# PSUM banks given back at their last reading, one pool for slabs and temporaries, and activation tables asked for early

## The chip, the cores and the metric

The kernel runs on one core of a Trainium2 chip. The metric is the time of one execution in microseconds of the device; three runs of the kernel before gave 800.99, 803.68 and 805.22, median 803.68 us. The core has TensorE (PE in the profile; PEld is its weight load), VectorE (DVE), ScalarE (ACT), GpSimd (POOL) and SyncE (SP), which issues nearly all transfers here. Products land in PSUM, which has eight banks of 128 x 512 fp32; everything else is held in SBUF.

## The reference

Two layers of a decoder trunk over 256 tokens of width 1024, fp32 in and out:

```
for i in range(2):
    h = rms_norm(x, norm_mix[i])
    x = x + (dsa_moba_mixer(h, ...) if i == 0 else nsa_mixer(h, ...))
    x = x + memory_cross_attention(rms_norm(x, norm_mem[i]), rms_norm(mem, norm_mem_src[i]), ...)
    x = x + swiglu(rms_norm(x, norm_ffn[i]), ffn_w_in[i], ffn_w_out[i])
```

- Mixer of layer 0: one projection of 2472 columns. Half A: an indexer of 8 small ReLU heads scores all causal keys, each query keeps its best 64, and 8 heads attend to those with one shared key and value head. Half B: 8 heads of plain causal attention (with 256 tokens there is one block). Queries and keys are RMS-normed per head and turned by rotary angles in 16 of 64 columns.
- Mixer of layer 1: 16 heads in 4 groups, three branches (15 compressed blocks, selected blocks, a window), each with its own keys and values, mixed by sigmoid gates; then an output projection.
- Memory attention: 4 heads of 128 columns over 256 memory rows. Feed-forward: SiLU(g) * u with 2816 columns.

## The kernel before

Tokens stand in two tiles of 128 (`t` = 0, 1). All large products are done in three passes of fp32r: `mm3` multiplies high by high, high by low and low by high part, so that one fp32 product has three TensorE instructions per 128 rows of the sum. Weights come in blocks of 256 x 512 fp32 (`raw`, three buffers), ScalarE or VectorE rounds them to a high part, and VectorE subtracts it for the low part (`whl`, six buffers).

Nothing is in a fixed order. Every step of the computation is a generator that yields one operation at a time (`Op`) or a condition; `Steps.run` collects the operations that are ready, asks a model of the engines (`Est`) when each could start, and issues the one that could start first, with a small window (`WAIT`) in which rank and age decide. So the instruction order of each engine is the outcome of a planner. What moves an instruction is when its generator is let on (a buffer or a flag) and what the model believes of durations and of the TensorE clock.

Buffers are `Slots`: a tile is taken with `get` (which waits until one is open) and given back by calling the function that came with it. PSUM has four such sets of two banks: `MM` (`mm`, the large products), `SP` (`sp`, scores), `TP` (`tp`, transposes) and `PV` (`po`, values). In SBUF there are 23 slabs (`SL`), and of temporaries four `T2` (`t2`), two `T4`, three `SN` (`sn`, scores), four `PT` (`pt`, transposed scores) and two `GV` (`gv`); `T2` and `T4` both read `t` in the profile. Giving back is the planner's act: on the chip the next writer of a bank waits by semaphore for its last reader, whenever the planner gave it back.

`gemm` takes a bank of `MM`, issues the product and starts an evacuation `ev`. The evacuations of queries and keys (`ev_q`, `ev_k`, `ev_sw`) copy the bank to a temporary and then run `inv_rms`, whose first step squares the bank on ScalarE:

```
yield move(q.rearrange("p h d -> p (h d)"), ps)
yield from inv_rms(ps, 8, HD, (yield from root("mix0", t))[0], 1.0, HD, rq[j, t])
free()
```

`inv_rms` goes on to a sum on VectorE, a scale-and-add on VectorE and a power on GpSimd; the bank is given back after these.

In layer 0 the products come in the order `s` (indexer, shared key and value), `aq`, `bk`, `bq`, `bv`, then `mk` (memory keys) and `out`; in layer 1 `kc`, `ks`, `kw`, `vw`, `q0`, `q1`, then `mk` and `out`. The attention generators run beside them. `tables` computes the rotary sines and cosines (`ang`, `sin`, `cos`) and the norm gains that TensorE spreads over the partitions in one small product. In the profile all instructions of an engine's helper are on line 238, so tiles tell them apart, not lines.

Of the kernel before, what the change touches and what calls it, by code (L numbers as in the profile page):

```python
# [53 lines left out]
NSLAB = 23  # L54
TAPS = 8
PTS = 4


class Op:
# [81 lines left out]
class Est:  # L141


    def __init__(self, nc):
        self.clk = {"PE": 0.0, "V": 0.0, "S": 0.0, "G": 0.0, "D": 0.0, "port": 0.0}
        self.wr, self.rd, self.busy = {}, {}, {}
        self.thin = False
        self.now = 0.0
        self.eng = {n: Est.Engine(self, n, e) for n, e in
                    (("PE", nc.tensor), ("V", nc.vector), ("S", nc.scalar), ("G", nc.gpsimd))}  # L150
# [44 lines left out]

    def issue(self, e, outs, ins, cost):
        lock = self.locks(e, outs, ins)
        t = max(self.clk[e], self.after(e, outs, ins), self.clk["port"] if lock else 0.0)
        if e == "PE":
            w = int(t / 3.413)  # L200
            c = cost * (1 if self.busy.get(w - 1, 0.0) > 1.26 else 2)
            n = 1
            for d in outs[0].shape[1:]:
                n *= d
# [12 lines left out]
        for a in outs:  # L217
            self.note(a, self.wr, t, e)

    class Engine:  # L220
# [3 lines left out]
        def __getattr__(self, name):  # L224
            f = getattr(self.e, name)

            def call(*a, **k):
                aps = [v for v in (*a, *k.values()) if hasattr(v, "tensor")]
                outs, ins = [aps[0]], aps[1:]
                if name == "tensor_tensor_reduce":  # L230
                    outs.append(aps[-1])
                    ins = aps[1:-1]
                elif k.get("accum_out") is not None:
                    outs.append(k["accum_out"])
                    ins = [v for v in ins if v is not k["accum_out"]]

                def do():
                    return f(*a, **{q: v() if q in ("start", "stop") and callable(v) else v for q, v in k.items()})  # L238
                return Op(self.est, [(self.n, outs, ins, self.cost(name, a, k, outs, ins), do)])
            return call  # L240

        def cost(self, name, a, k, outs, ins):
# [56 lines left out]

@with_exitstack  # L300
def trunk(ctx: ExitStack, tc: tile.TileContext, I, out):
# [37 lines left out]
    spawn = ck.spawn  # L339
    MM, SP, TP, PV = Slots(est, pp, "mm", 2), Slots(est, pp, "sp", 2), Slots(est, pp, "tp", 2), Slots(est, pp, "po", 2)  # L340
# [131 lines left out]
    PO.memset(one, 1.0).issue()  # L472
    mhalf = cp.tile([P, 16], F32, name="mhalf")
# [18 lines left out]
    def tables():  # L492
# [20 lines left out]
        yield S.activation(cos, ang, AF.Sin)  # L513
        yield has(("mix0", 0), 2)
# [254 lines left out]
    def mixer0():  # L769
# [119 lines left out]
        def ev_k(ps, free, t):  # L889
# [3 lines left out]
            yield from inv_rms(ps, 8, HD, (yield from root("mix0", t))[0], 1.0 / HD, 1.0, rk)  # L893
            free()
# [98 lines left out]
    def mixer1():  # L993
# [92 lines left out]
        def ev_sw(br):  # L1086
            def ev(ps, free, t):
# [7 lines left out]
                free()  # L1095
# [28 lines left out]
        def ev_q(j):  # L1124
            def ev(ps, free, t):
                q, qf = yield from T2.get([P, 8, HD])
                yield move(q.rearrange("p h d -> p (h d)"), ps)
                yield from inv_rms(ps, 8, HD, (yield from root("mix1", t))[0], 1.0, HD, rq[j, t])
                free()
# [160 lines left out]
    def mem_k(L):  # L1290
# [3 lines left out]
        def ev(ps, free, t):  # L1294
# [3 lines left out]
            yield from inv_rms(ps, MH, MD, mvr[t][0], 1.0 / MD, 1.0, rk)  # L1298
            free()
# [15 lines left out]
    def mem_attn(L):  # L1315
        vm = hp.tile([P, NT, MH, MD], F32, name="mvm")
        qT, rq = {}, [hp.tile([P, MH], F32, name=f"mrq{t}") for t in range(NT)]

        def ev_q(ps, free, t):
            q, qf = yield from T2.get([P, MH, MD])  # L1320
            yield S.activation(q.rearrange("p h d -> p (h d)"), ps, AF.Copy)
            yield from inv_rms(ps, MH, MD, (yield from root(("mem", L), t))[0], 1.0, MD, rq[t])
            free()
# [20 lines left out]
        def mem_pv(t, p, sp, spf, sn, snf):  # L1344
# [20 lines left out]
            for i in range(2):  # L1365
                yield together([T.matmul(po[:, i, :], vm[:, b, h0 + i, :], pt[:, 2 * i + b, :], start=(b == 0), stop=(b == 1))
                                for b in range(2)])
            ptf()
            hl, hf = yield from SL.get([P, 2, 2, P], F32R)
# [4 lines left out]
        def ev_v(p):  # L1374
            def ev(ps, free, t):
                yield move(vm[:, t, 2 * p:2 * p + 2].rearrange("p h d -> p (h d)"), ps, mvr[t][1])
# [183 lines left out]
```

## Time and profile before

| | us |
|---|---|
| median of three runs | 803.68 |
| profiled execution | 802.33 |
| its span on the core | 800.6 |
| TensorE busy | 765.6 (96%) |
| VectorE busy | 533.0 (67%) |
| ScalarE busy | 436.7 (55%) |
| GpSimd busy | 132.8 (17%) |
| SyncE's queue moved | 120.5 MB |

The profile's span leaves out 1.7 us around the program. The page gives for each engine how long it worked; the stretches give the same between two times, with the clock granted to TensorE as a share of full speed; the timeline gives instructions in order, with the idle time ahead of them and what ended it. An engine's idle time matters where it is on the path that sets the end.

### The profile page before, as it was taken

The numbers are of one execution on the slowest core, as the hardware profiler recorded it, in microseconds if no ns is written. First come the engines' busy times: TensorE is split into PE (matmuls) and PEld (weight loads), VectorE is DVE, ScalarE is ACT, GpSimd is POOL, SyncE is SP. The second block draws the span as 40 slices with busy tenths as digits, with TensorE's granted clock in tenths as the row PEclk, the third lists the DMA queues.
The fourth block names the chain that finished last, engine by engine and source line by source line (L and its number), as shares of the span: only waits on it lengthen the run. The fifth ranks groups of instructions, "written<-read, shape, count | busy, mean of one in ns | idle before, by whom it ended". The sixth has DMA issues, their size and how long they took to land.

```text
span 800.6 us, 11834 instructions
## 1 busy us (share of the span) xinstructions
PE 765.6 (96%) x4259; PEld 635.5 (79%) x4259; DVE 533.0 (67%) x1088; ACT 436.7 (55%) x822; POOL 132.8 (17%) x194
## 2 busy tenths in 40 slices
PE   6988999999999999999998988999999999999998
PEld 5766788897888889788877767887897888889886
DVE  6888998868555554554726888886857565546541
ACT  5766985675543443443615677884656344435430
POOL 1665340100000000000016373340200000000000
PEclk9998999999999999999999998999999999999999
DMA  7633643426556645876414623033624665546751
GB/s 221 192 98 92 194 136 100 142 102 193 166 171 206 186 156 157 228 247 186 131 46 123 212 78 106 2 105 108 188 102 132 211 187 183 160 140 212 218 189 52
DMA packets 69482, 121.27 MB, mean 151 GB/s; under 512 B 8420, under 2 KB 15664, under 8 KB 69424
## 3 DMA queue, kind: packets, MB, share of 16 engines
q1 hardware_dynamic: 69392, 120.53, 48.8%
q8 instruction: 33, 0.54, 0.3%
q14 instruction: 25, 0.20, 0.1%
q0 software_dynamic: 32, 0.00, 0.0%
HBM read 119.46 MB, written 1.05 MB: 151 GB/s over the span
## 4 chain that ended last, share of the span: by engine, by line
PE 78%; DVE 8%; ACT 5%; DMA 5%; issue 2%; POOL 1%; SPq 0%; ACTq 0%; DVEq 0%; POOLq 0%
PE mm L238 58%; PE po L238 11%; PE tp L238 7%; PE sp L238 2%; DVE whl L238 2%; DVE slab L238 1%; ACT whl L238 1%; DMA raw<-in_ffn_w_in 1%; DMA raw<-in_ab_w_in 1%; ACT sn L238 1%; DMA raw<-in_nsa_w_in 1%; ACT slab L238 1%; DVE sn L238 1%; DVE kvT L238 1%; DVE hss L238 1%
## 5 line engine op out<-in xcount | busy, mean ns | idle before, releaser
L238 PE MATMUL mm<-whl,h 128*128 128x512 f32 (+3 forms) x1776 | 399.1, 379 | 10.1 <-DVE whl L238 9.1
L238 PEld LDWEIGHTS mm<-whl,h 128*128 128x128 f32 x1776 | 311.8, 189 | 69.9 <-DVE whl L238 10.9
L238 DVE TENSOR_TENSOR whl<-raw,whl 128x1024 fp32r<-128x1024 f32 (+3 forms) x232 | 271.3, 1174 | 143.3 <-ACT whl L238 139.0
L238 ACT ACTIVATE whl<-raw 128x1024 fp32r<-128x1024 f32 (+2 forms) x212 | 214.7, 1016 | 167.4 <-DMA raw<-in_ffn_w_in 42.0
L238 PE MATMUL mm<-whl,slab 128*128 128x512 f32 (+1 forms) x840 | 198.6, 375 | 2.0 <-ACT mvm L238 1.0
L238 PEld LDWEIGHTS mm<-whl,slab 128*128 128x128 f32 x840 | 141.7, 188 | 28.3 <-DVE x L238 1.8
L238 PE MATMUL po<-whl,slab 128*128 128x512 f32 x264 | 68.2, 396 | 0.0
L238 POOL TENSOR_TENSOR rh<-vh,mhalf 128x1 f32<-128x1 f32 x12 | 10.1, 845 | 326.7 <-DVE vh L238 310.5
L238 ACT ACTIVATE slab<-tp 128x256 fp32r<-128x256 f32 (+2 forms) x72 | 31.3, 463 | 50.9 <-PE tp L238 50.8
L238 PEld LDWEIGHTS po<-whl,slab 128*128 128x128 f32 x264 | 49.3, 188 | 11.4
L238 ACT ACTIVATE sn<-sn,mx 128x128 f32<-128x128 f32 (+1 forms) x96 | 42.7, 448 | 6.2 <-DVE mx L238 5.8
L238 POOL TENSOR_TENSOR sn<-sn,rc 128x512 f32<-128x512 f32 (+2 forms) x32 | 32.6, 1022 | 48.9 <-DVE rc L238 30.8
L238 PE MATMUL tp<-ident,t 128*128 128x128 f32 x224 | 35.5, 282 | 4.4 <-DVE slab L238 2.9
L238 PEld LDWEIGHTS tp<-ident,t 128*128 128x128 f32 x224 | 27.3, 143 | 11.8 <-POOL t L238 3.2
L238 DVE CUSTOM_DVE_ANT_0 sn<-sp,cm,rq 128x128 f32<-128x128 f32 (+1 forms) x80 | 30.6, 409 | 7.8 <-PE sp L238 6.6
L238 PE MATMUL tp<-ident,sn 128*128 128x128 f32 (+1 forms) x180 | 31.6, 288 | 2.1 <-POOL sn L238 1.4
L238 ACT ACTIVATE pt<-tp 128x512 f32<-128x512 f32 (+2 forms) x51 | 26.8, 535 | 11.7 <-PE tp L238 11.1
L238 DVE TENSOR_TENSOR x<-mm,x 128x512 f32<-128x512 f32 x36 | 24.5, 686 | 13.0 <-PE mm L238 12.9
L238 ACT ACTIVATE h<-gv 128x512 fp32r<-128x512 f32 x22 | 13.8, 628 | 30.9 <-DVE gv L238 30.9
L238 ACT ACTIVATE t<-mm,rh 128x512 f32<-128x512 f32 (+1 forms) x26 | 17.0, 654 | 24.7 <-PE mm L238 24.7
L238 ACT ACTIVATE t<-mm 128x512 f32<-128x512 f32 (+2 forms) x44 | 23.1, 557 | 9.1 <-PE mm L238 6.9
L238 PEld LDWEIGHTS tp<-ident,sn 128*128 128x128 f32 (+1 forms) x180 | 21.8, 146 | 7.5 <-POOL sn L238 2.3
(198 smaller groups left out, 667.9 us busy)
## 6 DMA issues: line engine op xcount, KB each, us to landing
raw<-in_ffn_w_in SPq DMA_DIRECT2D x80, 512.0 KB, 3.9
raw<-in_ffn_w_out SPq DMA_DIRECT2D x44, 512.0 KB, 4.4
raw<-in_ab_w_in SPq DMA_DIRECT2D x16, 512.0 KB, 3.7
raw<-in_mem_w_kv SPq DMA_DIRECT2D x16, 512.0 KB, 3.8
raw<-in_nsa_w_in SPq DMA_DIRECT2D x16, 512.0 KB, 4.1
raw<-in_ab_w_out SPq DMA_DIRECT2D x8, 512.0 KB, 3.7
raw<-in_mem_w_q SPq DMA_DIRECT2D x8, 512.0 KB, 3.8
raw<-in_mem_w_o SPq DMA_DIRECT2D x8, 512.0 KB, 4.1
```

Of the source, the lines that this page charges most:

```text
L238: return f(*a, **{q: v() if q in ("start", "stop") and callable(v) else v for q, v in k.items()})
```

## The change

1. `inv_rms` gets the bank's `free` and calls it right after the square; in `ev_sw` the copy of the values is put ahead of it.
2. Slabs, `T2`, `SN`, `PT` and `GV` share one pool of 36 places of 2 KB. Each kind has a least number (23, 4, 3, 2, 1) that stays reserved for it; what is over goes to who asks first. The values of the memory attention (`mvm`, 4 KB of their own) now take two places.
3. A one-column activation with Sin is issued in the set-up, and one with Exp right behind the cosine.
4. The planner's model: ScalarE is charged 1.28 us when its table changes, the TensorE clock is believed to follow plain busy time, and an fp32 product of 64 x 64 weights is charged 0.235 us.

```
 class Op: issue
+        if e == "S":
+            self.est.load(getattr(f, "func", None))
         self.est.issue(e, outs, ins, cost)
 class Est
+    def load(self, func):
+        table = {AF.Sin: "sin", AF.Exp: "exp", AF.Silu: "silu"}.get(func)
+        if table not in (None, self.table):
+            self.table = table
+            self.clk["S"] += 1.28
     issue, TensorE
             c = cost * (1 if self.busy.get(w - 1, 0.0) > 1.26 else 2)
-            self.busy[w] = self.busy.get(w, 0.0) + cost * ins[0].shape[0] / P * min(1.0, n / P)
+            self.busy[w] = self.busy.get(w, 0.0) + cost
     cost, TensorE
+                if ins[0].shape[0] == 64 and outs[0].shape[0] == 64:
+                    return 0.235
+class Kind:
+    def ready(self):
+        p = self.p
+        if p.used[self.k] < p.least[self.k]:
+            return True
+        return len(p.slots.open) > sum(max(0, p.least[k] - p.used[k]) for k in p.least)
...
-    SL = Slots(est, hp, "slab", NSLAB)
-    T2, T4, SN, PT = Slots(est, tp, "t2", 4), Slots(est, tp, "t4", 2), Slots(est, tp, "sn", 3), Slots(est, tp, "pt", PTS)
-    GV = Slots(est, tp, "gv", 2)
+    places = Places(est, hp, "place", PLACES, LEAST)
+    SL, T2, SN, PT, GV = (places.kind(k) for k in LEAST)
+    T4 = Slots(est, tp, "t4", 2)
...
+    S.activation(warm, one, AF.Sin).issue()
...
         yield S.activation(cos, ang, AF.Sin)
+        yield from ready(AF.Exp)
...
-    def inv_rms(ps, H, dh, v, mul, add_k, r):
+    def inv_rms(ps, H, dh, v, mul, add_k, r, free):
         sq, f = yield from T2.get([P, H, dh])
         yield S.activation(sq.rearrange("p h d -> p (h d)"), ps, AF.Square)
+        free()
...
     ev_q of layer 0 (ev_k, ev_q of layer 1, mem_k and mem_attn alike)
-                yield from inv_rms(ps, 8, HD, (yield from root("mix0", t))[0], 1.0, HD, rq[j, t])
-                free()
+                yield from inv_rms(ps, 8, HD, (yield from root("mix0", t))[0], 1.0, HD, rq[j, t], free)
     ev_sw
-                yield from inv_rms(ps[:, :256], G, HD, v, 1.0 / HD, 1.0, rk[:, :G])
                 if br == 0:
                     yield S.activation(vv[:, t, :G, :], ps[:, 256:].rearrange("p (h d) -> p h d", h=G), AF.Copy, scale=r)
-                free()
+                yield from inv_rms(ps[:, :256], G, HD, v, 1.0 / HD, 1.0, rk[:, :G], free)
     mem_attn
-        vm = hp.tile([P, NT, MH, MD], F32, name="mvm")
+        vm = {}
...
+                if p == 0:
+                    vm[t] = yield from SL.get([P, MH, MD])
+                yield lambda: t in vm
```

The order moves on all engines in the two mixers; the same instructions stand in the same order in the feed-forward blocks. TensorE in layer 0, from the end of the second `bq` product to the `bv` product, before (`mm_753` and `mm_876` are these two products, `t_798`, `t_859` and `t_821` hold keys and a memory row tile):

```order
L238 MATMUL mm_753<-whl_689,h_113 128x512 x2
L238 MATMUL mm_753<-whl_689,h_114 128x512
L238 MATMUL tp_816<-ident,t_798 128x128 x4
L238 MATMUL tp_849<-ident,t_798 128x128 x4
L238 MATMUL tp_861<-ident,t_859 128x128 x4
L238 MATMUL mm_876<-whl_734,h_111 128x512 x2
```

Now, the same two products are `mm_764` and `mm_832`, the keys `t_804`:

```order
L245 MATMUL mm_764<-whl_696,h_115 128x512 x2
L245 MATMUL tp_812<-ident,t_804 128x128 x4
L245 MATMUL mm_764<-whl_696,h_116 128x512
L245 MATMUL mm_764<-whl_696,h_115 128x512 x2
L245 MATMUL mm_764<-whl_696,h_116 128x512
L245 MATMUL mm_832<-whl_736,h_113 128x512
L245 MATMUL tp_842<-ident,t_804 128x128 x4
```

The transposes that stood between the two products stand inside them.

TensorE in layer 1, where the first memory-key product (`mm_5104`, now `mm_5442`) sets in among the attention (`tp`, `po`, `sp`), before:

```order
L238 MATMUL tp_5063<-ident,sn_4989 128x128
L238 MATMUL po_4757<-pt_5041,vv 64x128 x4
L238 MATMUL po_4757<-pt_4987,vv 64x128 x4
L238 MATMUL tp_5063<-ident,sn_4989 128x128 x3
L238 MATMUL mm_5104<-whl_4462,slab_4969 128x512 x2
```

And now:

```order
L245 MATMUL tp_5382<-ident,place_5290 128x128
L245 MATMUL po_5264<-place_5376,vv 64x128 x4
L245 MATMUL po_5017<-place_5317,vv 64x128 x4
L245 MATMUL mm_5442<-whl_4483,place_5296 128x512
L245 MATMUL sp_5435<-place_4173,place_5187 128x256
```

From the last instruction of the `q1` products to this point 162 instructions stand without a product before, and 234 now; inside the second `q1` product 24 stood before and 81 stand now, so more of the attention is ahead of `mk`.

ScalarE at the sine and the cosine, before:

```order
L238 ACTIVATE whl_273<-raw_223 128x1024
L238 ACT_TABLE_LOAD
L238 ACTIVATE sin<-ang 128x16
L238 ACTIVATE whl_297<-raw_233 128x1024
L238 ACTIVATE t_304<-mm_241 128x424
L238 ACTIVATE sqk,ssk<-mm_241 128x64
L238 ACTIVATE cos<-ang 128x16
L238 ACTIVATE whl_314<-raw_271 128x1024
```

And now:

```order
L245 ACTIVATE sin<-ang 128x16
L245 ACTIVATE whl_299<-raw_235 128x1024
L245 ACTIVATE place_306<-mm_243 128x424
L245 ACTIVATE sqk,ssk<-mm_243 128x64
L245 ACTIVATE cos<-ang 128x16
L245 ACT_TABLE_LOAD
L245 ACTIVATE warm<-one 128x1
L245 ACTIVATE whl_354<-raw_297 128x1024
```

The load moves from ahead of the sine to behind the cosine; one conversion (`whl_314`) has gone to VectorE. Before, another load stands ahead of the first Exp of the attention; now none does. ScalarE has five loads in all for six.

## Rows read from the trace of the kernel before

**Rows 1.** The page: busy us (share) xinstructions of each engine; chain that ended last.

```profile
PE 765.6 (96%) x4259; PEld 635.5 (79%) x4259; DVE 533.0 (67%) x1088; ACT 436.7 (55%) x822; POOL 132.8 (17%) x194
...
PE 78%; DVE 8%; ACT 5%; DMA 5%; issue 2%; POOL 1%; SPq 0%; ACTq 0%; DVEq 0%; POOLq 0%
```

**Rows 2.** Stretches: length; TensorE, loads, VectorE, ScalarE, GpSimd busy (x); clock; DMA share, GB/s.

```profile
0.00:28.00 28.00, 19.07 (x84) 15.89 (x85) 18.98 (x59) 15.31 (x28) 5.53 (x14) 1.00 0.72 219
28.00:84.00 56.00, 48.69 (x240) 38.02 (x238) 48.34 (x135) 38.56 (x69) 33.63 (x60) 0.94 0.41 120
84.00:100.00 16.00, 15.91 (x94) 13.21 (x94) 15.71 (x52) 15.01 (x36) 5.97 (x6) 1.00 0.61 192
100.00:420.00 320.00, 318.24 (x1749) 263.43 (x1749) 200.63 (x332) 162.68 (x278) 22.39 (x32) 1.00 0.53 160
420.00:458.18 38.18, 33.07 (x195) 28.50 (x193) 28.95 (x60) 21.90 (x42) 17.82 (x29) 1.00 0.54 164
458.18:466.91 8.73, 8.73 (x53) 7.23 (x51) 7.18 (x27) 6.69 (x23) 8.65 (x11) 1.00 0.56 183
466.91:498.55 31.64, 25.07 (x213) 21.52 (x213) 25.93 (x96) 24.19 (x73) 14.16 (x19) 0.84 0.25 84
498.55:546.40 47.85, 47.79 (x394) 40.24 (x394) 37.99 (x143) 36.56 (x108) 17.08 (x20) 1.00 0.14 45
546.40:796.00 249.60, 248.19 (x1247) 207.13 (x1246) 148.54 (x193) 115.79 (x168) 7.55 (x8) 1.00 0.53 165
796.00:800.60 4.60, 0.80 (x4) 0.32 (x2) 0.69 (x1) 0.00 (x0) 0.00 (x0) 1.00 0.22 82
```

**Rows 3.** Short stretches, same columns.

```profile
66.94:70.77 3.83, 1.59 (x13) 1.36 (x12) 2.72 (x11) 2.64 (x6) 3.45 (x6) 0.96 0.21 86
476.00:480.00 4.00, 1.94 (x16) 1.51 (x15) 4.00 (x10) 2.97 (x11) 1.46 (x1) 1.00 0.34 131
480.00:484.00 4.00, 3.05 (x27) 2.87 (x28) 3.95 (x8) 2.04 (x4) 2.28 (x2) 0.51 0.53 152
476.00:488.00 12.00, 8.61 (x60) 7.47 (x59) 9.63 (x24) 6.75 (x19) 4.29 (x4) 0.72 0.60 203
```

**Rows 4.** TensorE in order: start, us, engine, line, what [idle before <- what ended it].

```profile
26.96 0.45 PE L238 MATMUL tp<-slab,one 76*128 76x112 f32 x2 [1.61 <-DVE slab L238]
...
70.21 0.91 PE L238 MATMUL tp<-ident,t 128*128 128x128 f32 x4 [2.24 <-DVE slab L238]
...
77.75 1.20 PE L238 MATMUL mm<-whl,h 128*128 128x512 f32 x4 [1.06 <-DVE whl L238]
```

**Rows 5.** TensorE in order, 420 to 458 us.

```profile
424.23 0.62 PE L238 MATMUL mm<-whl,h 128*128 128x256 f32 x3 [1.01 <-ACT vv L238]
...
431.98 1.09 PE L238 MATMUL mm<-whl,h 128*128 128x304 f32 x6 [0.76 <-DVE whl L238]
...
434.62 2.34 PE L238 MATMUL mm<-whl,h 128*128 128x304 f32 x15 [1.55 <-DVE whl L238]
...
443.65 8.29 PE L238 MATMUL mm<-whl,h 128*128 128x512 f32 x35 [1.34 <-DVE whl L238]
```

**Rows 6.** One stretch of a feed-forward block, columns as in rows 2.

```profile
260.00:280.00 20.00, 20.00 (x91) 16.45 (x90) 11.38 (x13) 9.35 (x11) 0.00 (x0) 1.00 0.59 185
```

**Rows 7.** ScalarE in order, around the sine table.

```profile
20.55 1.06 ACT L238 ACTIVATE whl<-raw 128x1024 fp32r<-128x1024 f32 x1 [1.09 <-DMA raw<-in_ab_w_in]
21.63 1.28 ACT L238 ACT_TABLE_LOAD   x1
22.92 0.22 ACT L238 ACTIVATE sin<-ang 128x16 f32<-128x16 f32 x1
...
25.71 1.06 ACT L238 ACTIVATE whl<-raw 128x1024 fp32r<-128x1024 f32 x1 [0.89 <-DMA raw<-in_ab_w_in]
```

**Rows 8.** VectorE in order, behind the sine.

```profile
23.17 0.18 DVE L238 TENSOR_TENSOR ang<-ang,turn 128x16 f32<-128x16 f32 x1 [1.78 <-ACT sin L238]
```

**Rows 9.** ScalarE in order, second reading of a product bank.

```profile
67.14 0.60 ACT L238 ACTIVATE t<-mm 128x512 f32<-128x512 f32 x1 [1.05 <-DVE hss L238]
```

More of the change, by code (lines that the diff above doesn't have):

```diff
@@ L53 @@
 AHEAD = 1
-NSLAB = 23
+PLACES = 36
+LEAST = {"slab": 23, "t2": 4, "sn": 3, "pt": 2, "gv": 1}
 TAPS = 8
-PTS = 4
 class Op:
@@ L147, in __init__ @@
         self.thin = False
+        self.table = None
         self.now = 0.0
@@ L297, in get, with __init__, kind, take @@
         return self.take(shape, dt)
+class Places:
+    def __init__(self, est, pool, name, n, least):
+        self.slots, self.least, self.used = Slots(est, pool, name, n), least, dict.fromkeys(least, 0)
+    def kind(self, k):
+        return Kind(self, k)
+class Kind:
+    def __init__(self, places, k):
+        self.p, self.k = places, k
+    def ready(self):
[3 more added lines that the diff above has]
+        return len(p.slots.open) > sum(max(0, p.least[k] - p.used[k]) for k in p.least)
+    def take(self, shape, dt=F32):
+        self.p.used[self.k] += 1
+        t, f = self.p.slots.take(shape, dt)
+        def free():
+            f()
+            self.p.used[self.k] -= 1
+        return t, free
+    def get(self, shape, dt=F32):
+        yield self.ready
+        return self.take(shape, dt)
 @with_exitstack
@@ L339, in trunk, with ready @@
     spawn = ck.spawn
+    warm = cp.tile([P, 1], F32, name="warm")
+    def ready(func):
+        yield S.activation(warm, one, func)
     MM, SP, TP, PV = Slots(est, pp, "mm", 2), Slots(est, pp, "sp", 2), Slots(est, pp, "tp", 2), Slots(est, pp, "po", 2)
-    SL = Slots(est, hp, "slab", NSLAB)
-    T2, T4, SN, PT = Slots(est, tp, "t2", 4), Slots(est, tp, "t4", 2), Slots(est, tp, "sn", 3), Slots(est, tp, "pt", PTS)
+    places = Places(est, hp, "place", PLACES, LEAST)
+    SL, T2, SN, PT, GV = (places.kind(k) for k in LEAST)
+    T4 = Slots(est, tp, "t4", 2)
     RP = Slots(est, tp, "rope", 3)
-    GV = Slots(est, tp, "gv", 2)
     flags = {}
@@ L892, in ev_k @@
             rk = tiny(8, "rk8")
-            yield from inv_rms(ps, 8, HD, (yield from root("mix0", t))[0], 1.0 / HD, 1.0, rk)
-            free()
+            yield from inv_rms(ps, 8, HD, (yield from root("mix0", t))[0], 1.0 / HD, 1.0, rk, free)
             yield from rope(q, 8, ra[:, t, 3], rb[:, t, 3], HALF)
@@ L1127, in ev @@
                 yield move(q.rearrange("p h d -> p (h d)"), ps)
-                yield from inv_rms(ps, 8, HD, (yield from root("mix1", t))[0], 1.0, HD, rq[j, t])
-                free()
+                yield from inv_rms(ps, 8, HD, (yield from root("mix1", t))[0], 1.0, HD, rq[j, t], free)
                 quT[t, j] = yield from SL.get([P, 4, P])
@@ L1297, in ev @@
             rk = tiny(MH, "mrk")
-            yield from inv_rms(ps, MH, MD, mvr[t][0], 1.0 / MD, 1.0, rk)
-            free()
+            yield from inv_rms(ps, MH, MD, mvr[t][0], 1.0 / MD, 1.0, rk, free)
             yield V.tensor_tensor(q, q, rk[:, :, None].to_broadcast([P, MH, MD]), op=OP.mult)
@@ L1321, in ev_q @@
             yield S.activation(q.rearrange("p h d -> p (h d)"), ps, AF.Copy)
-            yield from inv_rms(ps, MH, MD, (yield from root(("mem", L), t))[0], 1.0, MD, rq[t])
-            free()
+            yield from inv_rms(ps, MH, MD, (yield from root(("mem", L), t))[0], 1.0, MD, rq[t], free)
             qT[t] = (yield from SL.get([P, MH, P], F32R)), (yield from SL.get([P, MH, P], F32R))
@@ L1365, in mem_pv @@
             for i in range(2):
-                yield together([T.matmul(po[:, i, :], vm[:, b, h0 + i, :], pt[:, 2 * i + b, :], start=(b == 0), stop=(b == 1))
+                yield together([T.matmul(po[:, i, :], vm[b][0][:, h0 + i, :], pt[:, 2 * i + b, :], start=(b == 0), stop=(b == 1))
                                 for b in range(2)])
             ptf()
+            done(("mpv", L))
+            if has(("mpv", L), 2 * NT)():
+                for b in range(NT):
+                    vm[b][1]()
             hl, hf = yield from SL.get([P, 2, 2, P], F32R)
@@ L1375, in ev @@
             def ev(ps, free, t):
-                yield move(vm[:, t, 2 * p:2 * p + 2].rearrange("p h d -> p (h d)"), ps, mvr[t][1])
+                if p == 0:
+                    vm[t] = yield from SL.get([P, MH, MD])
+                yield lambda: t in vm
+                yield move(vm[t][0][:, 2 * p:2 * p + 2].rearrange("p h d -> p (h d)"), ps, mvr[t][1])
                 free()
```

5 lines of the change are left out of this document (1 added, 4 removed).

## The prediction

> **What bounds the kernel now.** I read the page first: busy shares, the granted clock, and the chain that ended last [rows 1]. TensorE is busy 765.6 of 800.6 us and holds 78% of the chain; VectorE has 67%, ScalarE 55%. The reader sees from this that nothing is to be had where TensorE has no gap, so I next cut the span into stretches [rows 2]: 84 to 420 and 546 to 796 us, the memory attentions and the feed-forward blocks, leave TensorE idle 3.3 us in 586 (0.09, 1.76 and 1.41). The changed program has the same 3967 TensorE instructions, form by form, and in the feed-forward blocks they stand in the same order. There I expect nothing.
>
> What can be won is the rest of the 35.0 us that TensorE is idle: 8.93 us in 0 to 28, 7.31 in 28 to 84, 5.11 in 420 to 458, 6.57 in 467 to 498.5, and 3.80 at the end, where the last store leaves. To it comes what the clock takes. It was 0.94 over 28 to 84 and 0.84 over 467 to 498.5 [rows 2], which is 0.06 x 56.0 = 3.4 and 0.16 x 31.64 = 5.1 us. It fell to 0.51, the lower of the two levels (1.2 of 2.4 GHz), in 480 to 484, after four microseconds of which TensorE was busy 1.94 [rows 3]; in 28 to 84 it fell after a stand of 2.24 us [rows 4]. The ceiling, all idle time but the store and all the clock, is 31.2 + 8.5 = 40 us, or 5%, and part of the 8.93 is the wait for the first inputs, which nothing here shortens.
>
> Last I asked what ends those waits. In 28 to 84 it is mostly transposes whose PSUM bank VectorE still reads, or converted weights that VectorE had not finished [rows 4]; in 420 to 458 it is converted weights, 3.65 of the 5.11 us [rows 5].
>
> **The change part by part, and the sum.** The sum is made against the profiled execution's 802.33 us, 1.35 below the median of the three runs (803.68). I subtract and then add the 1.35.
>
> *Banks given back at the last reading.* This removes no instruction. The planner lets the next product take a bank when the generator calls free; before, that came after two VectorE steps and the power on GpSimd; now it comes after the square on ScalarE. So the next product is placed earlier in TensorE's queue. In layer 0 the queue had twelve transposes and no product between the `bq` and `bv` products; now the next product follows at once. Before, TensorE went from 66.94 to 70.77 with 1.59 us of work [rows 3]. The work that then lies behind the products (the key and query preparation on ScalarE, VectorE and GpSimd) also starts earlier.
>
> How much of the 7.31 + 3.4 us in 28 to 84 comes back is set by VectorE, since index scores, selection and attention of this layer run there. VectorE is busy 48.34 of 56.0 us in that stretch and 15.71 of 16.0 in the next [rows 2]: it has 7.66 us to give before it is full, and that is the upper end. The lower end is below nothing. Between the last `bv` product and the first output product the order now has 148 TensorE instructions where there were 106, and 77 of VectorE for 41: TensorE's products have gone ahead, and what is left is attention that VectorE paces, with a run of 40 instructions without a product. Were VectorE to work in 84 to 100 at its share of 28 to 84 (86%, not 98%), the same 15.71 us would take 18.2, a loss of 2.2. I take a gain of 3.0, nearer to the middle of -2.2 and +7.7 than to the top because of what TensorE does up to the end of `bv` little has moved away: 342 instructions stand there for 380.
>
> In 420 to 458 (`kw`, `vw`, `q0`) the order now has 24 VectorE instructions between the first `kw` and the first `q0` product where it had 39: the key copies stand behind the weight conversions instead of ahead. The upper end is the whole idle time, 5.11; the lower is 0. The wait of 1.01 on `vv` [rows 5] I leave standing: that copy is only exchanged with the square behind it, and both still read the bank. I take 3.0.
>
> In 458 to 546 (last `q1` product, attention, `mk`, first output products) the two sides weigh most. Before, 48 instructions stand in the last `q1` product (8.73 us), then about 160 without a product (31.64 us), then 316 with `mk` and the output (47.85), 88.2 together [rows 2]. Now it is 105, 234 and 185. In the profile's counting, where an fp32 matmul that isn't a transpose has two records, the 234 are 326 records and the 160 were the 213 of the row. First and last part by TensorE: a 512-column product issues each 0.22 us (x91 fill 20 us with a few transposes between [rows 6]); the other records of the last row take (47.85 - 96 x 0.22) / 308 = 0.087 us. So 24 x 0.22 + 97 x 0.1 = 15 us and 96 x 0.22 + 125 x 0.087 = 32 us. The middle part has 100 VectorE instructions against 72. VectorE was 25.93 us busy for the 72; 100 are 36.0 us, the best case, and 43.9 at its share of then (82%). By TensorE's records at the old pace, 326 x 31.64 / 213 = 48.4, the worst. The part as a whole: 83, 91 and 95.4 us against 88.2, so from 5.2 gained to 7.2 lost. I take 40 for the middle part, between the first two, since more of these scores are in flight (temporaries are not limited to three any more) and the clock should fall less. 87 us: a gain of 1.0.
>
> *Tables asked for early.* The load of the sine table sat in front of the first sine: ScalarE ends a conversion at 21.61, loads until 22.91, and the sine starts at 22.92 [rows 7]; VectorE waits 1.78 us for it [rows 8], and behind it, through the rotary tables, TensorE waits 1.61 [rows 4]. Now the first load of the program is this table, while ScalarE waits for its first inputs. The Exp table comes in right after the cosine, about where the sine's load was; ScalarE then waits 0.89 us for weights [rows 7], which hides most of it. A VectorE weight conversion that is now placed before the rotary rows gives part of the 1.28 us back. 0 to 1.6; I take 1.0. The Exp load that stood before the first attention is gone too; its 1.28 us lie where TensorE has 0.09 us of gaps (84 to 100, [rows 2]), so I count it at nothing. If that cover is gone, it is 1.3 more.
>
> The Trainium skill says otherwise of such a load: "ScalarE: Activation LUTs", under "What ACT_TABLE_LOAD costs", adds a drain of about 1.38 us to 1.28 us of loading. In these rows 1.31 us pass from the conversion's end to the sine's start; the drain does not show. By the page the term would be 2.4 and the forecast 1.4 lower; the row decides.
>
> *One pool of places.* The 36 places are the 23 + 4 + 3 + 4 + 2 of before; the value rows of the memory attention now take two of them. No instruction comes or goes, and a place's next user waits for its last reader as before. Where the planner must wait for a place it shows in the order, and the terms above are from the order. Nothing for itself. The planner's own estimates (its busy account, 64x64 products, table loads) move instructions alone. Two tiny activations on a one-column tile and one table load fewer cost nothing that matters.
>
> Sum: 3.0 + 3.0 + 1.0 + 1.0 = 8.0. 802.33 - 8.0 = 794.3, and with 1.35 more 795.7 us. All upper ends give 19.6 us, all lower ends -9.4.
>
> **Rivals.** *VectorE is full anyway.* The products run ahead in layer 0 and the time comes back as the product-free run before the output products. For it: 98% in 84 to 100. Against it: 7.66 us free before. Term 0 there, half of the second (1.5), -0.5 for the third, 1.0 for the table: 2.0, so 801.7 us.
>
> *The product-free run of layer 1 grows and the clock with it falls.* For it: 326 records where there were 213, `mk` is placed later, and this is where the clock was 0.84. From 476 to 488 us 60 records took 12 us, 0.2 each [rows 3]. If half of the run goes at that pace and half at the old 0.149, it takes 326 x 0.174 = 57 us, the part 104, a loss of 15.8: 1 + 3 + 3 - 15.8 = -8.8, so 812.5 us. Slower by half a per cent it is once the run exceeds 52 us. Against it: more scores are in flight, and VectorE's share bounds the run at 44. "TensorE: Matmul & The Clock Gate" of the Trainium skill, under "HAM oscillation", says that gaps between bursts throttle the clock and that each burst after a gap starts at half rate; the drop to 0.51 after 476 to 480 agrees.
>
> *The earlier free is bookkeeping.* The bank's last reader is the same square; if ScalarE comes to it no earlier, the product stands at the head of the queue and waits there, now with the transposes behind it. For it: ScalarE's second read of a bank was at 67.14 after 1.05 us of waiting [rows 9]. Against it: ScalarE has 17 us free in 28 to 84, and the square now stands right behind the copy. Table 1.0 alone: 802.7 us.
>
> **How the numbers follow.** Forecast 0.60, own range 790 to 799.5; full VectorE 0.18; bookkeeping 0.10; product-free run 0.12. Half a per cent, about what a measurement here can tell, is 4.0 us: below 799.7 is faster, above 807.7 slower. The forecast is all faster, the two middle cases the same, the last slower: 0.60, 0.28, 0.12. The range 787 to 806 takes in both middle cases and cuts the last one and the far end of the sum.
>
> **What would show it.** In the changed profile: no TensorE gap over 1 us between 60 and 80 us and a clock of 1.00 there; VectorE above 90% in 28 to 84; no table load between the cosine and the feed-forward block; waits on converted weights in 420 to 458 under 2 us; and the run from the last `q1` to the first `mk` product 36 to 44 us long. I am wrong if TensorE's idle time stays near 35 us, or if that run exceeds 48.

## The result and the profile after

The changed kernel takes 794.09 us (median of 4 runs, 792.43 to 795.96) where the kernel before takes 802.77 (median of 4, 800.99 to 805.22). The ratio is 0.989, with a 95% interval of 0.9854 to 0.9926. Forecast were 795.7 us. The profiled execution took 792.43 us, 790.7 of them span. It is 1.66 us under its median, and the one of before was 0.44 under its own. So 9.9 us between the two traces stand for 8.7 between the medians.

The page after (busy us, share, instructions; then the chain by engine):

```profile
PE 760.4 (96%) x4259; PEld 630.9 (80%) x4259; DVE 529.8 (67%) x1088; ACT 428.7 (54%) x816; POOL 146.3 (19%) x201
...
PE 75%; DVE 10%; ACT 6%; DMA 4%; issue 3%; POOL 1%; SPq 0%; ACTq 0%; POOLq 0%; DVEq 0%
```

TensorE's busy time is 760.4 us for 765.6 and its idle time 790.7 - 760.4 = 30.3 for 35.0 [rows 1]. More than half of the 9.9 us (5.2) is therefore not waiting that went. It is the same 3967 instructions done in less time, with a granted clock of 1.000 over the whole span, where it was 0.989.

To see where the time went I cut both spans at the first instruction of the same products, which the order of TensorE's instructions gives. The columns are "start" to the first `aq` product; layer 0, from there to the first `mq` product; `mq` to `kc`, the memory attention and feed-forward block of layer 0 (up to the small transpose just ahead of `kc`); `kc` to the second `q1` product; from there to the end of the third output product of layer 1, where the equal part begins; and the rest. "Run" is the product-free run from the end of `q1` towards `mk`, with the granted clock in it; it stops 0.5 to 2.5 us short of the first `mk` product in E1, E2, E4, E7, E11 and E12, which changes no low-clock time in it. E1 to E12 are the experiments below.

| us | start | layer 0 | mq to kc | kc to q1 | q1 to out | rest | span | run | clock in run |
|---|---|---|---|---|---|---|---|---|---|
| before | 22.21 | 126.04 | 236.73 | 73.20 | 88.22 | 254.20 | 800.6 | 31.64 | 0.84 |
| changed | 22.68 | 124.60 | 237.32 | 69.46 | 82.00 | 254.64 | 790.7 | 34.44 | 1.00 |
| E1 bank alone | 22.51 | 127.51 | 236.68 | 70.96 | 86.27 | 254.77 | 798.7 | 26.22 | 0.93 |
| E2 pool alone | 22.80 | 124.82 | 241.36 | 72.67 | 82.21 | 254.84 | 798.7 | 38.16 | 1.00 |
| E3 tables alone | 22.52 | 127.50 | 236.94 | 73.12 | 85.52 | 254.50 | 800.1 | 28.85 | 0.94 |
| E4 three scores | 23.02 | 127.63 | 240.77 | 69.49 | 85.99 | 254.20 | 801.1 | 28.14 | 0.94 |
| E5 no estimates | 22.67 | 123.60 | 240.90 | 71.32 | 83.24 | 254.67 | 796.4 | 42.54 | 1.00 |
| E6 no bank | 22.21 | 124.48 | 238.33 | 72.82 | 83.54 | 254.22 | 795.6 | 42.67 | 1.00 |
| E7 no pool | 22.10 | 122.78 | 236.04 | 68.95 | 85.17 | 254.56 | 789.6 | 27.57 | 0.94 |
| E8 less VectorE | 22.65 | 120.22 | 237.96 | 69.47 | 82.47 | 254.63 | 787.4 | 34.44 | 1.00 |
| E9 changed again | 21.98 | 124.84 | 238.06 | 69.44 | 81.37 | 255.21 | 790.9 | 34.44 | 1.00 |
| E10 four temporaries | 21.97 | 130.57 | 238.63 | 70.37 | 81.42 | 254.24 | 797.2 | 34.46 | 1.00 |
| E11 no pool again | 22.08 | 122.60 | 235.56 | 69.16 | 85.49 | 254.51 | 789.4 | 27.59 | 0.94 |
| E12 five scores | 23.24 | 124.05 | 236.14 | 69.51 | 88.41 | 254.55 | 795.9 | 38.19 | 0.87 |

Two pairs in it are one program each (changed and E9, E7 and E11). In layer 0, `kc` to `q1` and `q1` to out they agree within 0.7 us. E3 has TensorE's order of before, yet layer 0 differs by 1.5 us and `q1` to out by 2.7, in the latter with another clock. So I take differences of 2 us and more for the order's, or of 1 us where the clocks are alike. "Start" moves by 0.7 us from one execution to the next.

From before to changed the columns differ by +0.47, -1.44, +0.59, -3.74, -6.22 and +0.44, together -9.9. The rows after that answer to [rows 2] (columns as there):

```profile
28.00:84.00 56.00, 51.59 (x262) 40.77 (x261) 48.94 (x121) 38.17 (x69) 39.74 (x60) 1.00 0.45 137
84.00:100.00 16.00, 13.93 (x77) 11.23 (x78) 16.00 (x67) 11.01 (x27) 4.30 (x6) 1.00 0.41 132
100.00:132.10 32.10, 30.27 (x242) 24.22 (x242) 29.88 (x102) 25.77 (x79) 15.71 (x17) 1.00 0.31 100
419.53:454.06 34.53, 32.88 (x194) 28.34 (x194) 25.43 (x54) 22.88 (x45) 19.84 (x30) 1.00 0.62 184
470.50:504.94 34.44, 30.78 (x327) 26.56 (x325) 32.17 (x141) 31.60 (x107) 20.65 (x24) 1.00 0.26 88
492.00:496.00 4.00, 2.55 (x31) 1.94 (x29) 3.90 (x10) 3.66 (x17) 2.28 (x3) 1.00 0.20 25
504.94:536.06 31.12, 30.92 (x212) 25.04 (x211) 22.04 (x60) 20.29 (x47) 7.92 (x9) 1.00 0.22 68
```

In layer 0 the clock is 1.00 now, but VectorE is busy all 16.00 us of 84 to 100 and TensorE only 13.93, where it had 15.91. What TensorE won before 84 us it gives back there. From `kw` to `q1` it stands 1.65 of 34.53 us (5.11 of 38.18 before). In the run it works 89% of the time, against 79% before, and VectorE 93% against 82%. In the barest four microseconds of the run (492 to 496) TensorE was busy 2.55 us and the clock stayed at 1.00; before, it fell behind four of which 1.94 were busy [rows 3], and once more in the same run, at 469.8, behind four with 2.72.

TensorE's waits of 0.95 us and more in layer 0 after, answering to [rows 4], and then those on weights from `kw` to `q1`, answering to [rows 5] (start, us, line, instruction, idle time before and what ended it):

```profile
27.37 0.45 PE L245 MATMUL tp<-place,one 76*128 76x112 f32 x2 [1.07 <-DVE place L245]
...
39.51 0.30 PE L245 MATMUL tp<-ident,di 128*128 128x128 f32 x1 [1.03 <-ACT place L245]
...
69.36 0.95 PE L245 MATMUL mm<-whl,h 128*128 128x512 f32 x3 [1.01 <-DVE whl L245]
...
73.61 0.74 PE L245 MATMUL mm<-whl,h 128*128 128x512 f32 x2 [0.97 <-DVE whl L245]
...
94.70 0.71 PE L245 MATMUL sp<-place,place 128*128 128x256 f32 x4 [1.63 <-DVE mx L245]
```

```profile
428.98 2.75 PE L245 MATMUL mm<-whl,h 128*128 128x304 f32 x18 [0.20 <-DVE whl L245]
...
436.50 1.44 PE L245 MATMUL mm<-whl,h 128*128 128x512 f32 x5 [0.31 <-DVE whl L245]
...
439.51 7.38 PE L245 MATMUL mm<-whl,h 128*128 128x512 f32 x31 [0.90 <-DVE whl L245]
```

The wait behind the rotary tables is 1.07 us where it was 1.61, the one of 2.24 us on a transpose's bank is gone, the one of 1.06 on converted weights is still there as 1.01 and 0.97, and new ones have come: 1.03 us on ScalarE at 39.51 and 1.63 us on a score's maximum at 94.70, where VectorE is full. From `kw` to `q1` the four waits of [rows 5], 0.76 to 1.55 us, have shrunk to 0.90 at most.

ScalarE's first three table loads after [rows 7]:

```profile
0.79 1.28 ACT L245 ACT_TABLE_LOAD   x1 [0.79 <-PEq L1604]
...
24.98 1.28 ACT L245 ACT_TABLE_LOAD   x1
...
200.97 1.28 ACT L245 ACT_TABLE_LOAD   x1
```

### The profile page after: what moved, and what is told of

Same layout as the page of the kernel before. It is cut to its first block, busy times and chain, and to the rows that moved or that the text cites. A ratio compares the mean times of both kernels' runs of the same rounds, so it can differ in the third digit from the quotient of the medians.

```text
span 790.7 us, 11806 instructions
## 1 busy us (share of the span) xinstructions
PE 760.4 (96%) x4259; PEld 630.9 (80%) x4259; DVE 529.8 (67%) x1088; ACT 428.7 (54%) x816; POOL 146.3 (19%) x201
## 4 chain that ended last, share of the span: by engine, by line
PE 75%; DVE 10%; ACT 6%; DMA 4%; issue 3%; POOL 1%; SPq 0%; ACTq 0%; POOLq 0%; DVEq 0%
PE mm L245 56%; PE po L245 11%; PE tp L245 6%; ACT place L245 3%; DVE whl L245 3%; DVE place L245 3%; PE sp L245 2%; ACT whl L245 2%; DMA raw<-in_ffn_w_out 1%; DMA raw<-in_ffn_w_in 1%; DVE kvT L245 1%; DMA x<-in_x 1%; DMA raw<-in_mem_w_kv 1%; DVE rc L245 1%; DMA raw<-in_nsa_w_in 1%
## 5 line engine op out<-in xcount | busy, mean ns | idle before, releaser
L245 ACT ACTIVATE whl<-raw 128x1024 fp32r<-128x1024 f32 (+3 forms) x209 | 211.4, 1014 | 165.6 <-PE mm L245 44.0
L245 PE MATMUL mm<-whl,place 128*128 128x512 f32 (+1 forms) x840 | 194.9, 374 | 2.3 <-DVE x L245 1.2
L245 PEld LDWEIGHTS mm<-whl,place 128*128 128x128 f32 x840 | 142.2, 188 | 29.6 <-ACT whl L245 1.4
L245 ACT ACTIVATE place<-tp 128x256 fp32r<-128x256 f32 (+4 forms) x123 | 57.3, 492 | 65.7 <-PE tp L245 65.5
L245 PE MATMUL po<-whl,place 128*128 128x512 f32 x264 | 68.0, 395 | 0.0
L245 PEld LDWEIGHTS po<-whl,place 128*128 128x128 f32 x264 | 49.3, 188 | 11.3
L245 PE MATMUL tp<-ident,place 128*128 128x128 f32 (+1 forms) x340 | 53.0, 276 | 5.1 <-DVE place L245 1.9
L245 PEld LDWEIGHTS tp<-ident,place 128*128 128x128 f32 (+1 forms) x340 | 39.0, 141 | 14.8 <-POOL place L245 3.9
L245 ACT ACTIVATE place<-place,mx 128x128 f32<-128x128 f32 (+1 forms) x96 | 42.6, 449 | 5.4 <-DVE mx L245 4.7
L245 POOL TENSOR_TENSOR place<-place,rc 128x512 f32<-128x512 f32 (+2 forms) x37 | 34.3, 934 | 26.9 <-DVE rc L245 19.8
L245 DVE TENSOR_TENSOR x<-mm,x 128x512 f32<-128x512 f32 x36 | 24.5, 684 | 12.2 <-PE mm L245 12.2
```

## The experiments

Each was timed beside the kernel before; E1 to E4, E5 to E8 and E9 to E12 each on one chip with the same runs of before (802.81, 802.64 and 801.65 us).

**E1, the bank alone**, on the kernel before:

```diff
     yield S.activation(sq..., ps, AF.Square)
+    free()
...
-    yield from inv_rms(...); free()
+    yield from inv_rms(..., free)
```

> The kernel before with one part of the change: the product's PSUM bank is given back right after the square. The prediction put 3.0 us of layer 0 and 3.0 us of the stretch from kw to q0 down to this part. By it: 6 us faster, 796.8 us against 802.8. Theory of the pool (the larger gains come from the pool of places, the earlier bank pays only where the keys of kw wait): the 3.7 us that the stretch from kw to q1 became shorter come, layer 0 and the run without a product of layer 1 stay as before, so about 799 us, and the clock between q1 and mk stays near 0.84.

Measured: 800.82 us, ratio 0.9982 (0.9964 to 1.0001). Layer 0 did not get shorter (127.51 us, as in E3), although the first `bv` product now starts at 65.4 us where it started at 70.8. `kc` to `q1` got 2.2 us shorter. My 3.0 for layer 0 does not show in the bank alone, the 3.0 for `kw` to `q0` holds within 1 us.

**E2, the pool alone**:

```diff
-    SL, T2, T4, SN, PT, GV = separate Slots of 23, 4, 2, 3, 4, 2
+    places = Places(est, hp, "place", 36, LEAST); SL, T2, SN, PT, GV = (places.kind(k) for k in LEAST)   # T4 stays by itself
```

> The kernel before with the pool of 36 places alone; banks, tables and the planner's estimates as before. By the prediction (the pool is worth nothing for itself): 802.8 us, the same as before. Theory of the pool: the last q1 product to the output products of layer 1 is 6 us shorter, with TensorE's clock at 1.00 between q1 and mk where it was 0.84, and the last bv product of layer 0 ends some 10 us earlier without the output products coming more than 1 us earlier: about 796 us.

Measured: 800.17 us, ratio 0.9967 (0.9949 to 0.9984). Layer 1 did what the theory said: `q1` to out is 6.0 us shorter, with a longer run at full clock (its row; before it was 31.64 us at 0.84, [rows 2]):

```profile
471.84:510.00 38.16, 33.76 (x351) 29.19 (x349) 36.06 (x154) 34.73 (x122) 22.42 (x27) 1.00 0.22 70
```

But `mq` to `kc` is 4.6 us longer, all of it in the feed-forward block, in which TensorE's order is that of before. Between `mq` and `kc` TensorE waits four times (5.3 us):

```profile
212.93 0.66 PE L248 MATMUL tp<-ident,place 128*128 128x128 f32 x4 [1.29 <-DVE place L248]
...
323.89 0.44 PE L248 MATMUL tp<-ident,place 128*128 128x128 f32 x2 [1.03 <-DVE place L248]
...
340.41 1.43 PE L248 MATMUL mm<-whl,place 128*128 128x512 f32 x5 [0.62 <-DVE whl L248]
...
380.28 0.66 PE L248 MATMUL tp<-ident,x 128*128 128x128 f32 x4 [2.38 <-DVE x L248]
```

The last one is a residual sum that stands on VectorE behind two conversions of the next layer's weights, whose loads came late. E4 and E5 are as long there (240.8 and 240.9), E6 to E12 are not (235.6 to 238.6). Yet in the feed-forward block E4 has the changed kernel's order on TensorE, ScalarE and VectorE, and E2 and E5 differ from it by one weight conversion, which is on ScalarE as before and has gone to VectorE in the changed kernel. From `mq` to `kc` ScalarE waits 32.6, 33.3 and 30.6 us for the weights of the down projection in E2, E4 and E5, and 25.6 and 28.1 in the two executions of the changed kernel. Why these loads land later in the three is not settled; E2 and E5 also lose some 1.5 us ahead of the down projection.

**E3, the tables alone**:

```diff
+S.activation(warm, one, AF.Sin).issue()
...
+    yield from ready(AF.Exp)      # behind the cosine
```

> The kernel before with the two early activations alone; the order of TensorE's instructions stays that of before. By the prediction the sine's load is worth 1.0 us (0 to 1.6): 801.8 us. Rival: what comes earlier up to the bk products is lost again where VectorE is full in layer 0 (84 to 110 us): 802.8 us. In the trace: no table load between 20 and 23 us and the first rotary work 1.3 us earlier in both cases.

Measured: 802.21 us, ratio 0.9997 (0.9979 to 1.0015): no change that can be measured. VectorE's wait for the sine fell from 1.78 to 0.47 us, but the next load took it back. ScalarE, and then VectorE, in order:

```profile
25.04 0.21 ACT L248 ACTIVATE cos<-ang 128x16 f32<-128x16 f32 x1
25.26 1.28 ACT L248 ACT_TABLE_LOAD   x1
26.55 0.20 ACT L248 ACTIVATE warm<-one 128x1 f32<-128x1 f32 x1
26.66 1.04 ACT L248 ACTIVATE whl<-raw 128x1024 fp32r<-128x1024 f32 x1
```

```profile
22.56 0.18 DVE L248 TENSOR_TENSOR ang<-ang,turn 128x16 f32<-128x16 f32 x1 [0.47 <-ACT sin L248]
...
27.74 1.23 DVE L248 TENSOR_TENSOR whl<-raw,whl 128x1024 fp32r<-128x1024 f32 x1 [0.83 <-ACT whl L248]
```

The Exp load stands ahead of a weight conversion that was ready, and VectorE waits 0.83 us for that conversion; `aq` to `bk` takes 14.03 us, with 13.41 before. I had hidden this load behind a wait of 0.89 us for weights that was no longer there. In the changed kernel the planner charges the load 1.28 us and gives that conversion to VectorE; `aq` to `bk` is 12.55. It takes 12.2 to 13.0 us in every run with the new estimates (changed, E4, E6 to E12) and 13.3 to 14.0 in every run without them (before, E1 to E3, E5). So early tables without the estimates gave nothing here; no run has the estimates without the tables, and how the 0.9 us divides between the two is not shown.

This run also shows what the clock costs, since its order of TensorE is that of before. The run between `q1` and `mk`:

```profile
468.88:497.73 28.85, 22.75 (x213) 19.31 (x213) 25.01 (x96) 24.01 (x74) 14.52 (x19) 0.94 0.25 92
```

It took 28.85 us at 0.94, where before took 31.64 at 0.84: 2.8 us less, where (1 - clock) x length is 5.06 - 1.73 = 3.3 us less.

**E4, three score temporaries** in the changed kernel:

```diff
     def ready(self):
+        if p.used[self.k] >= {"sn": 3}.get(self.k, 99): return False
```

> The changed kernel, but with at most three score temporaries in use at a time, as before; the rest of the pool stays. Theory of the pool: it is the score temporaries that pay in layer 1, so the 6 us between the last q1 product and the output products are lost and the clock there falls again to about 0.84: 800 us against 794.1. Rival (the other temporaries or the earlier banks pay): within 1 us of 794.1, clock 1.00.

Measured: 802.7 us, ratio 1.0008 (0.9987 to 1.003). The whole gain is gone. In the traces 4.0 us of it are in `q1` to out, where the clock fell, though less than I said (0.94):

```profile
471.94:500.08 28.14, 22.48 (x210) 18.93 (x211) 26.72 (x103) 23.82 (x75) 10.81 (x13) 0.94 0.33 113
```

3.0 are in layer 0, which I had not expected, and 3.5 in `mq` to `kc` (see E2).

**E5, the planner's estimates of before** in the changed kernel:

```diff
-    self.busy[w] = self.busy.get(w, 0.0) + cost
+    self.busy[w] = self.busy.get(w, 0.0) + cost * ins[0].shape[0] / P * min(1.0, n / P)
...
-    if ins[0].shape[0] == 64 and outs[0].shape[0] == 64: return 0.235
...
-    if e == "S": self.est.load(...)
```

> The changed kernel with the planner's estimates of before (busy account, 64 x 64 products, no charge for table loads); bank, pool and tables as changed. The prediction counted the estimates at nothing for themselves: within 1 us of 794.1. Rival: the parts only add up (bank alone -2.0, pool alone -2.6, tables alone -0.6 against 802.8), 797.6 us, and the rest of the 8.7 us comes from the estimates.

Measured: 797.45 us, ratio 0.9932 (0.9909 to 0.9956). The rival's figure: without the estimates it takes some 3 us more. In the trace the losses lie in `kc` to `q1` (1.9), `q1` to out (1.2) and `mq` to `kc` (3.6, the unsettled part), and layer 0 gains 1.0; the two traces are 5.7 us apart, the medians 3.4. So how much of the 3 us is the estimates' own, and how much the late loads, is open. I had counted the estimates at nothing.

**E6, the bank kept as before** in the changed kernel (the diff of E1, reversed).

> The changed kernel with the bank kept until after the power on GpSimd, as before. By the prediction's terms the bank carries 3.0 us in layer 0 and 3.0 in kw to q1: 800.1 us. Theory after the first runs (the bank pays in kw to q1 alone, 2 to 4 us; layer 0 is set by VectorE, the run before mk by the score temporaries): 796 to 798 us, kc to q1 longer by 2 to 4 us, the rest as in the changed kernel.

Measured: 797.31 us, ratio 0.9934 (0.9911 to 0.9957). `kc` to `q1` is 3.4 us longer and layer 0 the same (124.48). TensorE's waits there are those of [rows 5] again:

```profile
424.24 0.61 PE L245 MATMUL mm<-whl,h 128*128 128x256 f32 x3 [1.02 <-ACT vv L245]
...
431.97 1.11 PE L245 MATMUL mm<-whl,h 128*128 128x304 f32 x6 [0.73 <-DVE whl L245]
434.61 3.63 PE L245 MATMUL mm<-whl,h 128*128 128x304 f32 x15 [1.54 <-DVE whl L245]
```

The wait on `vv`, which I left standing, goes with the bank too. The run is the longest of all, and yet at full clock:

```profile
468.57:511.24 42.67, 37.97 (x392) 33.17 (x390) 40.21 (x174) 40.12 (x140) 24.36 (x28) 1.00 0.17 63
```

**E7, no pool** in the changed kernel (the diff of E2, reversed).

> The changed kernel with the separate places of before. Theory of the pool: the 6 us between the last q1 product and the output products of layer 1 are lost and the clock there falls, kc to q1 stays short: 800 us. By the prediction (the pool is worth nothing, the planner's other parts move the instructions): 794.1 us. By what the pool gave alone (2.6): 796.7 us.

Measured: 791.35 us, ratio 0.986 (0.9838 to 0.9881). The theory of the pool has the total the wrong way round. `q1` to out is 3.2 us longer and the clock in the run is lower, as it said, but layer 0 is 1.8 shorter and `mq` to `kc` 1.3.

**E8, less work for VectorE in layer 0**; the order stays that of the changed kernel. It leaves out most low parts of these weights (TensorE's products read the 32 columns again and again), so it is a probe and no version to keep:

```diff
-    yield V.tensor_tensor(u.lo, raw, u.hi, subtract)
+    # weights of bv, mk and out of layer 0: columns 0 to 31 only
+    yield V.tensor_tensor(u.lo[:, :, :32], raw[:, :, :32], u.hi[:, :, :32], subtract)
```

> The changed kernel in the same order of instructions, but the second weight conversion on VectorE writes only 32 of 512 columns for the weights of bv, mk and the output of layer 0 (16 pairs), and TensorE's products read these 32 again and again; the low parts of these weights are left out otherwise. This takes about 16 us from VectorE between 50 and 125 us and nothing from TensorE. Theory (VectorE, 98% busy there, sets the end of layer 0): TensorE's waits on VectorE between 60 and 133 us go, 4 to 6 us of the 6.7 it stands there, so 788 to 790 us. Rival (TensorE and the chain from score to product set it): within 1.5 us of 794.1.

Measured: 789.08 us, ratio 0.9836 (0.9811 to 0.986). Layer 0 is 4.4 us shorter than in the changed kernel. VectorE has room again (13.03 of 16.00, 20.20 of 27.54):

```profile
84.00:100.00 16.00, 14.43 (x89) 11.78 (x87) 13.03 (x63) 11.96 (x36) 5.04 (x8) 1.00 0.39 130
100.00:127.54 27.54, 26.14 (x216) 21.05 (x213) 20.20 (x85) 22.30 (x66) 11.70 (x13) 1.00 0.32 97
```

So VectorE's work sets the end of layer 0 in the changed kernel, as the rival had it.

**E9, the changed kernel again.**

> The changed kernel once more, so that it stands on one chip beside the three that follow: 794.1 us and 8.7 us under the kernel before, as in the first comparison. If its first profile (790.7 us of span) was one of its faster executions, the stages that vary from run to run are the down projections; the run from q1 to the output products of layer 1 stays at 82 us.

Measured: 794.26 us, ratio 0.9906 (0.9891 to 0.992).

**E10, four query, key and square temporaries** (E4's diff with `"t2": 4`).

> The changed kernel, but with at most four of the query, key and square temporaries in use at a time, as before; score temporaries and the rest share the pool. Theory: in layer 0 the extra temporaries of this kind only let products run ahead of VectorE and cost 1.8 us (aq to mq 122.8 us without the pool, 124.6 with it), in layer 1 the score temporaries save 3.2 us: 790 to 792 us. Rival: these temporaries pay in layer 0, then 795 us or more.

Measured: 797.06 us, ratio 0.9938 (0.9924 to 0.9952). The rival's figure, and more: in the trace layer 0 is 5.7 us longer than in E9, and 8 longer than without any pool. The profiled execution is the slowest of the six (798.95 us), 6.3 us over that of E9, where the medians are 2.8 apart. Around `bv` the clock fell in it, behind a wait of 2.48 us on converted weights; (1 - clock) x length is 3.5 us there:

```profile
65.36:90.32 24.96, 19.60 (x92) 15.23 (x90) 20.92 (x52) 14.58 (x27) 11.02 (x14) 0.86 0.33 97
```

```profile
73.15 0.51 PE L246 MATMUL mm<-whl,h 128*128 128x512 f32 x1 [2.48 <-DVE whl L246]
...
80.49 5.29 PE L246 MATMUL mm<-whl,h 128*128 128x512 f32 x15 [1.43 <-DVE whl L246]
```

**E11, no pool again**, beside E9.

> The changed kernel without the pool, beside the changed kernel on one chip. If the pool costs more than it gives once the banks, the tables and the estimates are changed, this is 2 to 3 us faster than the changed kernel (791.4 against 794.1); if that difference was one of chips, within 1 us of it.

Measured: 792.57 us, ratio 0.9882 (0.9869 to 0.9896), 1.7 us under E9; the intervals of the two overlap a little. Of the versions that do all the work this is the fastest, by little; leaving the pool out won 2.7 us in E7, against the first timing of the changed kernel, and 1.7 here.

**E12, five score temporaries and two for their transposes, without the pool.**

```diff
-    SN, PT = Slots(est, tp, "sn", 3), Slots(est, tp, "pt", 4)
+    SN, PT = Slots(est, tp, "sn", 5), Slots(est, tp, "pt", 2)
```

> The changed kernel without the pool, with five score temporaries and two for their transposes (before: three and four) in the same space. Theory (more scores in flight shorten the run before mk in layer 1): 3 us under the kernel without the pool, 788 us. Rival (in layer 0, where VectorE is full, more scores in flight only delay the output products): 791 us or more.

Measured: 794.76 us, ratio 0.9911 (0.9891 to 0.993), 2.2 us over E11. In the profiled execution, the slowest of the six (797.57 us), the run got longer and the clock in it fell:

```profile
468.61:506.80 38.19, 31.83 (x293) 28.27 (x293) 31.51 (x128) 31.14 (x103) 19.86 (x22) 0.87 0.26 83
```

The two of its six executions with a clock of 1.00 over the whole span took 792.22 and 792.58 us, as much as E11 and not the 788 of the theory; the four others, at 0.994 to 0.996, took 794.66 to 797.57. So five score temporaries did not help by themselves here. That speaks against the theory behind E4, though E12 also has two places fewer for the transposed scores.

## Why the prediction came out right

**The total held, two of its four terms did not.** Forecast gains were 3.0 (layer 0), 1.0 (sine table), 3.0 (`kw` to `q0`) and 1.0 (`q1` to out). The traces give 1.0 for the first two together (1.44 less 0.47 at the start), 3.7 and 6.2, and a loss of 1.0 in parts that I held for equal. Errors of 3.0 and 1.0 us one way and of 5.2 and 0.7 the other nearly cancelled: that the total came so near is luck.

The signs that I named came out so: no wait over 1.01 us in 60 to 80 and a clock of 1.00 there (right but for the 0.01), VectorE at 87% in 28 to 84 and not above 90 (wrong), no table load from the Exp at 24.98 to the feed-forward block's at 200.97 (right), 1.4 us of waits on converted weights in the stretch from `kw` to `q1` (right), TensorE's idle time 30.3 and not near 35 us (right), a run of 34.44 us, not 36 to 44 (short of it).

**Layer 0.** The step that failed is "I take a gain of 3.0", in the middle of the bounds. The 7.66 us that VectorE had free in 28 to 84 were no room for TensorE: VectorE's busy time there went from 48.34 to 48.94. The products ran ahead, `bv` ended 10.7 us earlier (83.9 for 94.7), and 9.7 of these were paid back before the end of the third output product. That is the rival "VectorE is full anyway", and E8 shows it. Nor was it the bank alone that let them run ahead: `bv` ended at 87.4 us with the bank alone (E1) and at 83.0 with the pool alone (E2). E1 and E6 show no gain of layer 0 by the bank.

**`kc` to `q1`.** Right, by 0.7 us too low. E6 puts 3.4 of the 3.7 us on the bank; alone (E1) it gave 2.2. The 1.0 us on `vv` came on top.

**`q1` to out.** This is the term that was mis-sized: 82.0 us, below even my best case of 83. First, 36.0 us for VectorE's 100 instructions came from the mean of the 72 before; the ones that joined were shorter, and it was busy 32.17 us. The middle part took 34.4 us, not 40, the first 16.4 for 15. The last took 31.1 for 32, with 84 products and not the 96 of my sum. Second, I wrote that the clock "should fall less" and put no price on it. In before (1 - clock) x length is 0.16 x 31.64 = 5.1 us. Taking that product away from the rows of the table leaves 83.2 (before), 82.0 (changed), 84.4 (E1), 82.2 (E2), 83.8 (E3, E11), 84.3 (E4), 83.2 (E5), 83.5 (E6, E7), 83.4 (E12) and 81.4 to 82.5 (E8 to E10): 3 us from end to end, where the column itself has 7. Most of what tells these orders apart goes with the clock, and the length of the run does not set it: runs of 34 to 43 us kept 1.00, but for E12, and those of 26 to 32 us did not. What divides them is the temporaries: with three for scores the clock in the run was 0.84 to 0.94 (before, E1, E3, E4, E7, E11), with the pool and no such limit 1.00 (changed, E2, E5, E6, E8, E9, E10); E12, with five and no pool, had 0.87. The rival "the product-free run of layer 1 grows and the clock with it falls" named the wrong cause. The run did grow, from 213 to 327 records, and nothing fell; what TensorE did before the fall in the kernel before was to stand (1.94 us of work in the four, [rows 3]), not to go without products. "TensorE: Matmul & The Clock Gate" of the Trainium skill, under "HAM oscillation", speaks of gaps between bursts and not of the kind of instruction. The rows agree; that a stretch without products must bring such gaps was my addition.

**Tables.** The 1.0 came out in the changed kernel (0.9 in `aq` to `bk`), together with the estimates, and was wrong as a part by itself (E3). No drain shows there either: 1.30 us pass from the cosine's end to the next activation in E3. By the page of the Trainium skill that the prediction named ("ScalarE: Activation LUTs", "What ACT_TABLE_LOAD costs") it would be 1.28 + 1.38 = 2.66.

**Pool and estimates.** "Nothing for itself" is wrong for the pool in both tests: alone it won 2.6 us (E2), and the finished kernel is 1.7 to 2.7 us faster without it, by a gain in layer 1 and larger losses ahead of it (E7, E11). For the estimates E5 speaks against it, with the open point named there. The parts alone give 2.0 (bank), 2.6 (pool) and 0.6 (tables), of which only the pool's is clear of the noise, 5.2 of 8.7 us together; the estimates were not tried alone. Taking one away costs 3.2 (bank) or 3.4 (estimates), and for the pool it wins.

**What stays open.** Why a limit on one kind of temporary inside the pool (E4, E10) costs more than taking the whole pool away, and why the loads of the down projection land later in E2, E4 and E5.

## What to carry to other kernels

When a list scheduler writes the order, its parts do not add: take each one out of the finished kernel as well as trying it alone, and read the result by stage, since one order may win 3 us in one stage and lose 2 in the next. Before a gap of one engine is counted as a gain, ask which engine's work lies behind it until the next equal point; if that one is 98% busy there, the gap only moves. Price a stretch with a lowered clock apart from its waits, as (1 - clock) x length: that was 5.1 of the 9.9 us between the two traces. Then see how much of it is paid. Over the 35 executions of the kernel before beside E1 to E4 (granted clock 0.985 to 0.998) a straight line gives 3.6 us of time for each 0.01 of clock, where the product is 8; over the six of E12 it gives 7.6. The median clocks of before and changed (0.991 and 0.999) are 0.008 apart, which is 3 us of the 8.7 by the line of before and 6 by the product: an estimate.

## What the runs showed of the hardware

A run without a product kept a granted clock of 1.00 over 42.67 us (E6), and a shorter one of 26.22 us had 0.93 (E1): it is not the missing products that lowered the clock here. The same order of TensorE had 0.84 in one execution and 0.94 in another (before and E3), 2.8 us apart. With one order of TensorE, ScalarE and VectorE in the feed-forward block, the part from `mq` to `kc` took 237.3 us in the changed kernel and 240.8 in E4, with 25.6 and 33.3 us of ScalarE's waits on the weights of the down projection. VectorE at 16.00 us of 16.00 made TensorE's earlier products worthless: `bv` ended 10.7 us earlier, and 1.0 us of it was left at the end of the third output product.
